# Gated delta rule in a hybrid backbone: z is projected with channels on partitions, its gate moves behind a transposition, and the products get a second kq buffer

## The chip, the cores and the metric

The kernel runs on one core of one Trainium2 chip. The metric is the device time of one execution in microseconds (us), as the median of several runs. The unchanged kernel took 2639.82 us (median of three runs, 2637.79 to 2641.33). The engines are called PE (matrix multiplication), PEld (its weight loads), DVE (vector), ACT (activation), POOL (GpSimd) and SP (which only issues DMAs here).

## The reference

Two layers over 2048 latent tokens and 256 context tokens of 1024 channels. The even layer has two branches behind one input projection: a bidirectional chunked gated delta rule (4 heads of 128 channels) and grouped attention. The change touches the delta rule's gate input z (columns 1536 to 2047 of the projection) and what multiplies it at the end:

```
pl = hl @ w_in
qkv_l, za_l, a_l, b_l, qb_l, kb_l, vb_l, zb_l = split_cols(pl, EVEN_SPLITS)
...
oa_l, _, _ = bidir_gdn(qa_l, ka_l, va_l, ga_l, ba_l, s_f, s_b, True)
...
def gdn_out(o, z, norm_g):
    bsz, nh, t, dv = o.shape
    o = rms_norm(o.transpose(0, 2, 1, 3), norm_g)
    y = o * jax.nn.silu(z.astype(F32).reshape(bsz, t, nh, dv))
    return y.reshape(bsz, t, nh * dv).astype(z.dtype)
```

## The kernel before

Every large product is split into a high and a low part and summed from three matmuls per 128 input channels (`mm3`, lines 133 to 138), so one output tile takes 24 of them.

The stages that matter follow each other in the program; a scheduler (the tile framework, with a timeline model of its own) then fixes one order of instructions per engine, and each engine works through its own list in that order. PE, for one, cannot pass over a matmul that waits.

**Projection "b"** (`b_item`, L517): tokens on partitions. 128 tokens are the stationary operand, 256 weight columns move. It is called for a/b/q, k, q and then for z: 2 column halves by 16 token tiles are 32 z items. A z item ends in Tanh on ACT (L554), a fused add and multiply on DVE (L555), the norm's gain `gg` on POOL (L557, tile zg) and a store to `d_zg` (L558).

**Projection "zb"** (`zb_item`, L604): the attention branch's gate, with channels on partitions. 128 weight columns are stationary, 512 tokens move; 4 heads by 4 token blocks are 16 items, each with Tanh (L612), DVE (L613) and a store.

**Products** (`gdn_products`, L785): for each of 18 chunks of 128 tokens (two of them context), what the recurrence needs and what does not depend on its state. For each direction d: two groups of four ACT scalings build gm from the high and the low part of the log decay (L796), two matmuls sum them into psg (L801, L802), four ACT exponentials give dm (L805), POOL masks it (L806). The matmuls of k with k and q (psk, L815) read tile kq, loaded from DRAM (L777), and DVE multiplies psk by dm into ntA and atA (L817, L819), which are stored. The ring of dm has two buffers, that of gm two, that of kq one. The products are emitted between the z items (`[prod] * 5` per item, L392).

**Substitution** (`gdn_subst`, L828): inverts 32 by 32 blocks of the chunks' triangular matrices, in 31 steps of one multiplication (sbT, L857) and one reduction on DVE (sbC, L858). Pass 0 runs on DVE; from pass 1 on, the steps after the twelfth multiply on POOL. Passes 0 and 1 are emitted beside z and zb, passes 2 to 4 (`late_subst`) beside attention. Pass 2 needs the last chunks' products.

**Mix** (`layer0_mix`, L619): attention, the recurrence (`gdn_chain`, L932, with `gdn_final`, L999) and the late substitution, merged. Attention starts with scores ps_s, which need khi (an ACT cast of the keys) and klo (DVE, L147). The keys' split lies in memory that the products release, and DVE casts three pieces of vhi ahead of klo. A final adds both directions' outputs (POOL, L1005), forms the norm, multiplies zg by it (POOL, L1015) and the output by that (POOL, L1016), transposes (PE, L1020), copies to yt (ACT, L1022) and stores. Tile yt shares a ring of three buffers ("ry") with r and y of the recurrence.

After that come the output projection, the second layer with its convolution, and its output; the change does not touch them.

Of the kernel before, what the change touches and what calls it, by code (L numbers as in the profile page):

```python
# [8 lines left out]
F32 = mybir.dt.float32  # L9
# [98 lines left out]
class Build:  # L108
# [44 lines left out]
    def setup(self, es):  # L153
# [29 lines left out]
        self.d_zg = d("d_zg", [NT, P, H * P])  # L183
# [103 lines left out]
    def layer0_in(self):  # L287
        tc, nc = self.tc, self.nc
        with ExitStack() as es:
# [67 lines left out]
            with tc.tile_pool(name="stB", bufs=2, reuse_waits="tile") as st:  # L357
                self.gq = st.tile([P, P], F32, name="gq", bufs=1)
                self.gk = st.tile([P, P], F32, name="gk", bufs=1)
                nc.sync.dma_start(self.gq, self.i["ev_q_norm_g"][0].partition_broadcast(P))  # L360
                nc.sync.dma_start(self.gk, self.i["ev_k_norm_g"][0].partition_broadcast(P))
                late = self.ada_late([(1, 4), (1, 5)], lambda: st.tile([P, 512], F32, tag="stage", name="ada_part2"))
                blks = [(2048, 272, "abq"), (2576, 256, "k"), (2320, 256, "q"), (1536, 256, "z")]
                items = []
                for (c0, n, kind), nxt in zip(blks, blks[1:]):
                    shared = {}
                    if kind == "q":
                        self.pipe(items)
                        items = []
                        e4.close()  # L370
                        self.es_mix = em = ExitStack()
                        cp = em.enter_context(tc.tile_pool(name="mixc", bufs=1, side="right", reuse_waits="tile"))
                        self.mix_consts(cp)
                        self.gg = cp.tile([P, P], F32, name="gg", bufs=1)
                        nc.sync.dma_start(self.gg, self.i["ev_gdn_norm_g"][0].partition_broadcast(P))
                        nc.vector.tensor_scalar(out=self.gg, in0=self.gg, scalar1=0.5, scalar2=None, op0=ALU.mult)
                        self.gates(cp)
                    for tt in range({"abq": NT + 1, "k": NTA}.get(kind, NT)):
                        items.append(self.b_item(c0, n, kind, tt, st, None, nxt[:2] if tt == 8 else None, shared))
                        if LATE_T(tt, kind):  # L380
                            items.append(late)
                self.pipe(items)
                self.pipe([late])
            with tc.tile_pool(name="stZ", bufs=2, reuse_waits="tile") as st:
                self.sub = em.enter_context(tc.tile_pool(name="subst", bufs=1, side="right", reuse_waits="tile"))
                with tc.tile_pool(name="prod", bufs=2, side="right", reuse_waits="tile") as gp:
                    prod = self.all_products(gp, self.tp)
                    subst = self.all_subst(range(2))
                    items = []
                    for c0, nxt in ((1536, (1792, 256)), (1792, (3088, P))):  # L390
                        for tt in range(NT):
                            items += [prod] * (0 if tt < Z_FREE and c0 == 1536 else 5) + [subst] * (SUB_Z if c0 > 1536 or tt >= 4 else 0)  # L392
# [124 lines left out]
    def b_item(self, c0, n, kind, tt, st, W=None, nxt=None, shared=None):  # L517
# [33 lines left out]
        if kind == "z":  # L551
            zs = st.tile([P, 2, P], F32, tag="wb", name="zs", bufs=4)
            z3 = body.rearrange("p (h c) -> p h c", h=2)
            nc.scalar.activation(zs, z3, AF.Tanh, scale=0.5)  # L554
            nc.vector.scalar_tensor_tensor(out=zs, in0=zs, scalar=1.0, in1=z3, op0=ALU.add, op1=ALU.mult)  # L555
            zg = st.tile([P, 2, P], F32, tag="wb", name="zg", bufs=4)
            nc.gpsimd.tensor_tensor(out=zg, in0=zs, in1=self.gg.unsqueeze(1).to_broadcast([P, 2, P]), op=ALU.mult)  # L557
            nc.sync.dma_start(self.d_zg[tt, :, c0 - 1536:c0 - 1536 + 256], zg)  # L558
            return
# [44 lines left out]
    def zb_item(self, hh, b, st, key, nxt):  # L604
# [9 lines left out]
        nc.sync.dma_start(self.d_szb[hh, :, b * 512:(b + 1) * 512], sz)  # L614
# [35 lines left out]
    def gates(self, cp):  # L650
# [134 lines left out]
    def gdn_products(self, c, gp, pp):  # L785
# [4 lines left out]
        for d in range(2):  # L790
# [7 lines left out]
            kq = kq or self.load_kq(c, gp, 1)  # L798
# [133 lines left out]
    def gdn_chain(self, d, c, n, W, done):  # L932
# [18 lines left out]
        else:  # L951
# [12 lines left out]
        nc.scalar.copy(y, py)  # L964
# [34 lines left out]
    def gdn_final(self, c, o):  # L999
# [4 lines left out]
        nc.sync.dma_start(zg, self.d_zg[c].rearrange("p (h c) -> p h c", h=H))  # L1004
# [10 lines left out]
        nc.gpsimd.tensor_tensor(out=zg, in0=zg, in1=rn.unsqueeze(2).to_broadcast([P, H, P]), op=ALU.mult)  # L1015
        nc.gpsimd.tensor_tensor(out=o, in0=o, in1=zg, op=ALU.mult)  # L1016
# [5 lines left out]
        nc.scalar.copy(yt, pt)  # L1022
# [517 lines left out]
```

## Time and profile before

| | us |
|---|---|
| median of three runs | 2639.82 |
| profiled execution, its own time | 2641.57 |
| its span | 2639.8 |
| first z Tanh (L554) starts | 637.2 |
| first zb weight load (L136, ps_zb) | 752.5 |
| first attention score (L136, ps_s) | 868.77 |
| last product of the recurrence's finals (L1016) starts | 1601.6 |
| last attention score starts | 1729.2 |

The profile page gives busy time, instructions and idle time by groups. A group's row reads: line, engine, operation, output<-inputs, shapes, count, then busy time and the mean duration of one in ns, then the engine's idle time just before these instructions and what ended most of it. Matmuls are pipelined: the duration of one reaches into the next one's, so two durations cannot be added; the distance from start to start can. A windows row gives for each engine the busy time and the count of instructions in a stretch, then the granted PE clock (1.00 is full speed), the DMA share and GB/s. A timeline row gives the start, the time from the first start to the last end of a run of equal instructions, the engine, the line, their count and in brackets the idle time before them.

### The profile page before, as it was taken

What the parts mean: (1) busy time and instruction counts of PE and PEld (TensorE: products, weight loads), DVE (VectorE), ACT (ScalarE), POOL (GpSimd) and SP (SyncE); (2) the same over time, 40 slices, a digit from 0 to 9 for tenths busy, and PEclk for the clock granted to TensorE, in tenths of its full rate; (3) what the DMA queues carried; (4) which work ended last, traced back from release to release, by engine and by line L of the source; (5) the groups of instructions that cost most, each with busy time, mean ns of one, the idle gap of its engine ahead of it and who ended that gap; (6) DMA issues with size and microseconds to landing.
All of it is one profiled execution on the core that took longest, in us unless ns stands there. A gap on an engine that the chain in (4) does not pass through costs nothing. (4 is left out here: it accounts for less than half of the span.)

```text
span 2639.8 us, 43225 instructions
## 1 busy us (share of the span) xinstructions
PE 2528.4 (96%) x15072; PEld 2206.1 (84%) x15072; DVE 2032.2 (77%) x4224; ACT 1457.2 (55%) x3033; POOL 1375.5 (52%) x1138
## 2 busy tenths in 40 slices
PE   7999999999999799999999999999999999999988
PEld 5888877998888688889989998887888888888767
DVE  8567667775855889897888777555489999997985
ACT  7444456224675665656566666444366667665332
POOL 3344433666445644361344324002179999897664
PEclk9999999999999899999999999999999999999989
DMA  8133334334566753545544434224311111116442
GB/s 313 49 122 101 109 112 130 107 102 152 164 195 203 202 122 109 147 116 139 158 116 129 125 96 132 63 81 142 136 49 56 56 60 61 56 64 213 151 158 100
DMA packets 372729, 323.21 MB, mean 122 GB/s; under 512 B 74784, under 2 KB 301600, under 8 KB 372512
## 3 DMA queue, kind: packets, MB, share of 16 engines
q1 hardware_dynamic: 372512, 320.46, 39.7%
q8 instruction: 119, 1.95, 0.3%
q14 instruction: 98, 0.80, 0.1%
HBM read 216.05 MB, written 104.33 MB: 121 GB/s over the span
## 5 line engine op out<-in xcount | busy, mean ns | idle before, releaser
L1410 DVE SCALAR_TENSOR_TENSOR pc<-u,hw,pc 128x1024 f32<-128x1024 f32 x320 | 389.7, 1280 | 5.1 <-ACT pc L1408 3.8
L1418 POOL TENSOR_TENSOR ac<-ac,pr 128x512 f32<-128x512 f32 x288 | 379.1, 1340 | 16.9 <-ACT ac L1414 6.2
L1121 ACT CAST phi<-pt 128x512 fp32r<-128x512 f32 x288 | 165.5, 585 | 157.1 <-PE pt L1117 145.3
L1417 ACT ACTIVATE pr<-u,hw 128x512 f32<-128x512 f32 x288 | 204.1, 721 | 84.8 <-POOL ac L1418 83.7
L1122 DVE TENSOR_TENSOR plo<-pt,phi 128x512 fp32r<-128x512 f32 x288 | 195.3, 685 | 60.0 <-ACT phi L1121 57.2
L136 PE MATMUL ps_b<-w_hi,hhi 128*128 128x256 f32 (+1 forms) x800 | 231.9, 292 | 9.6 <-DVE xn L571 6.1
L137 PE MATMUL ps_b<-w_lo,hhi 128*128 128x256 f32 (+1 forms) x800 | 228.0, 287 | 0.9 <-DVE w_lo L147 0.8
L138 PE MATMUL ps_b<-w_hi,hlo 128*128 128x256 f32 (+1 forms) x800 | 225.3, 287 | 0.6 <-POOL hlo L147 0.6
L1075 DVE TENSOR_SCALAR_CACHE_REDUCE S<-ps_s 128x512 f32<-128x512 f32 (+1 forms) x320 | 197.5, 630 | 23.3 <-PE ps_s L138 11.7
L1084 ACT ACTIVATE S<-S,m 128x1024 f32<-128x1024 f32 (+1 forms) x192 | 177.6, 928 | 61.3 <-DVE m L1081 60.8
L136 PE MATMUL ps_out<-wohi,yhi 128*128 128x512 f32 x512 | 204.2, 399 | 2.8 <-DVE x L1252 1.5
L138 PE MATMUL ps_out<-wohi,ylo 128*128 128x512 f32 x512 | 201.7, 395 | 0.7 <-DVE ylo L147 0.7
L137 PE MATMUL ps_out<-wolo,yhi 128*128 128x512 f32 x512 | 202.2, 395 | 0.0
L1145 PE MATMUL po<-phi,vhi 128*128 128x256 f32 x576 | 169.0, 315 | 12.4 <-ACT phi L1121 8.8
L1117 PE MATMUL pt<-ident,S 128*128 128x128 f32 x1152 | 174.1, 273 | 0.7 <-DVE plo L1122 0.5
L137 PE MATMUL ps_a<-hlo,w_hi 128*128 128x512 f32 (+1 forms) x448 | 170.7, 381 | 0.0
L136 PE MATMUL ps_a<-hhi,w_hi 128*128 128x512 f32 (+1 forms) x448 | 170.6, 381 | 0.0
L138 PE MATMUL ps_a<-hhi,w_lo 128*128 128x512 f32 (+1 forms) x448 | 170.1, 380 | 0.2 <-POOL w_lo L147 0.2
L477 DVE SCALAR_TENSOR_TENSOR acc<-ub,cols,acc 128x512 f32<-128x512 f32 (+1 forms) x168 | 136.5, 821 | 38.5 <-POOL acc L475 36.5
L136 PEld LDWEIGHTS ps_b<-w_hi,hhi 128*128 128x128 f32 x800 | 153.1, 192 | 13.1 <-issue 5.2
L857 POOL TENSOR_TENSOR sbT<-sbC 128x169 f32<-128x169 f32 (+18 forms) x76 | 120.2, 1582 | 77.9 <-DVE sbC L858 50.8
L137 PEld LDWEIGHTS ps_b<-w_lo,hhi 128*128 128x128 f32 x800 | 153.3, 192 | 2.4 <-DVE w_lo L147 1.8
(329 smaller groups left out, 7716.8 us busy)
## 6 DMA issues: line engine op xcount, KB each, us to landing
raw_ada<-in_ada_w_dram SPq DMA_DIRECT2D x48, 512.0 KB, 4.0
x<-in_x_dram SPq DMA_DIRECT2D x32, 512.0 KB, 7.7
kq<-d_kT SPq DMA_DIRECT2D x54, 256.0 KB, 3.4
raw_w<-in_ev_w_in_dram SPq DMA_DIRECT2D x26, 512.0 KB, 3.8
kq<-d_qT SPq DMA_DIRECT2D x48, 256.0 KB, 3.6
raw_w<-in_od_w_in_dram SPq DMA_DIRECT2D x24, 512.0 KB, 3.7
d_nt<-ntA SPq DMA_DIRECT2D x36, 256.0 KB, 3.3
nt<-d_nt SPq DMA_DIRECT2D x36, 256.0 KB, 4.4
```

Of the source, the lines that this page charges most:

```text
L136: self.nc.tensor.matmul(ps, lhsT=lh, rhs=rh, start=(a == 0), stop=False)
L137: self.nc.tensor.matmul(ps, lhsT=lh, rhs=rl, start=False, stop=False)
L138: self.nc.tensor.matmul(ps, lhsT=ll, rhs=rh, start=False, stop=(a == n - 1))
L1075: nc.vector.tensor_scalar(out=S[g][:, k0:k0 + w], in0=ps[:, :w], scalar1=1.0, scalar2=None, op0=ALU.mult, op1=ALU.max, accum_out=mx[:, b:b ...
L1084: nc.scalar.activation(S[g], S[g], AF.Exp, bias=m, scale=scale, accum_out=l[:, g:g + 1])
L1117: nc.tensor.transpose(pt[:, e, a * P:(a + 1) * P], S[a][k0 // 1024][:, k0 % 1024:k0 % 1024 + P], self.ident)
L1121: nc.scalar.copy(hi, pt)
L1122: nc.vector.tensor_tensor(out=lo, in0=pt, in1=hi.bitcast(F32), op=ALU.subtract)
L1145: nc.tensor.matmul(po, lhsT=vhi[:, ks], rhs=hi[:, e, :], start=(k == 0), stop=False)
L1410: nc.vector.scalar_tensor_tensor(out=pc, in0=s(j), scalar=w(j), in1=pc, op0=ALU.mult, op1=ALU.add)
L1417: nc.scalar.mul(pr, s(j), w(j))
L1418: nc.gpsimd.tensor_tensor(out=ac, in0=ac, in1=pr, op=ALU.add)
```

## The change

Four things are changed.

1. z is projected by `zb_item`, which takes its destination as an argument: 4 heads by 4 token blocks, 128 weight columns stationary and 512 tokens moving, 16 items in place of 32. `d_zg` holds channels by tokens. Between the items stand twice as many steps of the products and of the substitution. The norm's gain is no longer multiplied in here.
2. In `gdn_final` POOL multiplies o by the norm, PE transposes, ACT multiplies the transposed rows by the gain (now one value per partition) on its way out of PSUM, and POOL then multiplies yt by the gate.
3. kq has two buffers in the products.
4. Constants: the strict triangles are loaded apart and kept in one form, `negc` is gone (r takes the other sign, and y turns it back).

```diff
-        self.d_zg = d("d_zg", [NT, P, H * P])
+        self.d_zg = d("d_zg", [H, P, T])
...
-                    for c0, nxt in ((1536, (1792, 256)), (1792, (3088, P))):
-                        for tt in range(NT):
-                            items += [prod] * (0 if tt < Z_FREE and c0 == 1536 else 5) + [subst] * (SUB_Z if c0 > 1536 or tt >= 4 else 0)
-                            items.append(self.b_item(c0, 256, "z", tt, st, None, nxt if tt == 8 else None))
+                    zkey = [(1536 + hh * P, P) for hh in range(H)] + [(3088, P)]
+                    for n in range(4 * H):
+                        hh, b = n // 4, n % 4
+                        items += [prod] * (0 if n < 1 else 10) + [subst] * (2 * SUB_Z if n >= 2 else 0)
+                        items.append(self.zb_item(self.d_zg, hh, b, st, zkey[hh], zkey[hh + 1] if b == 2 else None))
...
-        if kind == "z":
-            zs = st.tile([P, 2, P], F32, tag="wb", name="zs", bufs=4)
-            z3 = body.rearrange("p (h c) -> p h c", h=2)
-            nc.scalar.activation(zs, z3, AF.Tanh, scale=0.5)
-            nc.vector.scalar_tensor_tensor(out=zs, in0=zs, scalar=1.0, in1=z3, op0=ALU.add, op1=ALU.mult)
-            zg = st.tile([P, 2, P], F32, tag="wb", name="zg", bufs=4)
-            nc.gpsimd.tensor_tensor(out=zg, in0=zs, in1=self.gg.unsqueeze(1).to_broadcast([P, 2, P]), op=ALU.mult)
-            nc.sync.dma_start(self.d_zg[tt, :, c0 - 1536:c0 - 1536 + 256], zg)
-            return
...
-            kq = kq or self.load_kq(c, gp, 1)
+            kq = kq or self.load_kq(c, gp, 2)
...
-                nc.vector.scalar_tensor_tensor(out=r[:, h, :], in0=pk[:, h, :], scalar=j(self.negc, h), in1=vt[:, h, :],
-                                               op0=ALU.mult, op1=ALU.add)
+                nc.vector.scalar_tensor_tensor(out=r[:, h, :], in0=pk[:, h, :], scalar=j(self.egc, h), in1=vt[:, h, :],
+                                               op0=ALU.mult, op1=ALU.subtract)
...
-        nc.scalar.copy(y, py)
+        nc.scalar.mul(y, py, 1.0 if S is None else -1.0)
...
-        nc.sync.dma_start(zg, self.d_zg[c].rearrange("p (h c) -> p h c", h=H))
+        nc.sync.dma_start(zg, self.d_zg[:, :, c * P:(c + 1) * P].rearrange("h p t -> p h t"))
...
-        nc.gpsimd.tensor_tensor(out=zg, in0=zg, in1=rn.unsqueeze(2).to_broadcast([P, H, P]), op=ALU.mult)
-        nc.gpsimd.tensor_tensor(out=o, in0=o, in1=zg, op=ALU.mult)
+        nc.gpsimd.tensor_tensor(out=o, in0=o, in1=rn.unsqueeze(2).to_broadcast([P, H, P]), op=ALU.mult)
...
-        nc.scalar.copy(yt, pt)
+        nc.scalar.mul(yt, pt, self.gg)
+        nc.gpsimd.tensor_tensor(out=yt, in0=yt, in1=zg, op=ALU.mult)
```

The edits move instructions on every engine's list. In the rows below a line number belongs to the version shown, and the numbers behind names tell buffers apart.

PE before, at the end of the stage: the last zb matmuls (ps_zb), then the last chunk's products (psg, psk) and attention's first scores (ps_s).

```order
L136 MATMUL ps_zb_10032<-hhi0_110,w_hi_9666 128x512
L802 MATMUL psg_9302<-gm_9257,strict_6329 128x512
L137 MATMUL ps_zb_10032<-hlo0_111,w_hi_9666 128x512
L138 MATMUL ps_zb_10032<-hhi0_110,w_lo_9667 128x512
L801 MATMUL psg_9321<-gm_9311,strict_6329 128x512
L815 MATMUL psk_9334<-kq_9262 128x256 x2
L815 MATMUL psk_9341<-kq_9262 128x256 x2
L802 MATMUL psg_9321<-gm_9316,strict_6329 128x512
L136 MATMUL ps_s_10127<-khi_9728,qhi_10121 128x512
```

PE now, from the last zb matmul on, down to the second of five chunks.

```order
L136 MATMUL ps_zb_9507<-hhi0_110,w_lo_9142 128x512
L793 MATMUL psg_8489<-gm_8481,strict_6329 128x512
L792 MATMUL psg_8508<-gm_8498,strict_6329 128x512
L806 MATMUL psk_8521<-kq_8486 128x256 x2
L806 MATMUL psk_8528<-kq_8486 128x256 x2
L793 MATMUL psg_8508<-gm_8503,strict_6329 128x512
L792 MATMUL psg_8552<-gm_8539,strict_6329 128x512
L793 MATMUL psg_8552<-gm_8544,strict_6329 128x512
L792 MATMUL psg_8618<-gm_8608,strict_6329 128x512
L806 MATMUL psk_8631<-kq_8549 128x256 x2
L806 MATMUL psk_8638<-kq_8549 128x256 x2
```

Before, two of the 72 psg matmuls and one of the 18 chunks' psk groups stood behind the last zb matmul. Now 19 psg matmuls and five psk groups stand there, and no projection lies between them. Ahead of that point, from the first psg on, each chunk's products have some 50 matmuls of 512 columns between them now; before, they had about 70 of 256 columns in z and 50 of 512 in zb.

ACT before, at the same place: the last two zb evacuations (szb), the last gm and dm groups, then the cast of the keys (khi).

```order
L612 ACTIVATE szb_10028<-ps_zb_10003 128x512
L796 ACTIVATE gm_9311<-cons_6327,ghi_6348 128x128 x4
L805 ACTIVATE dm_9305<-psg_9302,lnb_6343 128x128 x4
L796 ACTIVATE gm_9316<-cons_6327,glo_6349 128x128 x4
L612 ACTIVATE szb_10057<-ps_zb_10032 128x512
L805 ACTIVATE dm_9324<-psg_9321,lnb_6343 128x128 x4
L144 CAST khi_9728<-kraw_9730 128x1024
```

ACT now: the last szb and what follows it, and then the end of the same stretch.

```order
L602 ACTIVATE szb_9532<-ps_zb_9507 128x512
L796 ACTIVATE dm_8492<-psg_8489,lnb_6348 128x128 x4
L787 ACTIVATE gm_8503<-cons_6327,glo_6353 128x128 x4
L787 ACTIVATE gm_8539<-cons_6327,ghi_6352 128x128 x4
L796 ACTIVATE dm_8511<-psg_8508,lnb_6348 128x128 x4
L787 ACTIVATE gm_8544<-cons_6327,glo_6353 128x128 x4
```

```order
L851 COPY sbT_8164<-sbC_8163 128x1024
L796 ACTIVATE dm_8788<-psg_8785,lnb_6348 128x128 x4
L787 ACTIVATE gm_8821<-cons_6327,glo_6353 128x128 x4
L787 ACTIVATE gm_8879<-cons_6327,ghi_6352 128x128 x4
L796 ACTIVATE dm_8873<-psg_8870,lnb_6348 128x128 x4
L787 ACTIVATE gm_8884<-cons_6327,glo_6353 128x128 x4
L796 ACTIVATE dm_8892<-psg_8889,lnb_6348 128x128 x4
L840 ACTIVATE sbC_9621<-sbT_9622 64x1024
L142 CAST khi_9203<-kraw_9205 128x1024
```

Before, one dm group stood between the last szb and khi. Now ten dm groups, 17 gm groups, the copy at the end of substitution pass 1 (sbT<-sbC) and the first scaling of pass 2 (sbC<-sbT) stand there. POOL's list has, over the same stretch, dm and the last six multiplications of pass 1 (676 to 961 elements) in turn, then four dm.

POOL at a pair of finals, before: the norm (rno) and both multiplications, then the next W and the state's decay (S0, S1).

```order
L150 TENSOR_TENSOR rno_18780<-sso_18775,mhalf_64 128x4
L1015 TENSOR_TENSOR zgl_18771<-zgl_18771,rno_18780 128x512
L1016 TENSOR_TENSOR o_18472<-o_18472,zgl_18771 128x512
L150 TENSOR_TENSOR rno_18809<-sso_18804,mhalf_64 128x4
L881 TENSOR_TENSOR W_19321<-wc_19317,cons_6327 128x512
L1015 TENSOR_TENSOR zgl_18800<-zgl_18800,rno_18809 128x512
L1016 TENSOR_TENSOR o_18493<-o_18493,zgl_18800 128x512
L881 TENSOR_TENSOR W_19344<-wc_19340,cons_6327 128x512
L982 TENSOR_TENSOR S0_19804<-S0_19190,egt_6347 128x512
```

POOL now, at the same place.

```order
L148 TENSOR_TENSOR rno_18255<-sso_18250,mhalf_64 128x4
L1006 TENSOR_TENSOR o_17947<-o_17947,rno_18255 128x512
L148 TENSOR_TENSOR rno_18283<-sso_18278,mhalf_64 128x4
L872 TENSOR_TENSOR W_18796<-wc_18792,cons_6327 128x512
L1006 TENSOR_TENSOR o_17968<-o_17968,rno_18283 128x512
L872 TENSOR_TENSOR W_18819<-wc_18815,cons_6327 128x512
L1013 TENSOR_TENSOR yt_18465<-yt_18465,zgl_18246 128x512
L1013 TENSOR_TENSOR yt_18503<-yt_18503,zgl_18274 128x512
L973 TENSOR_TENSOR S0_19279<-S0_18665,egt_6351 128x512
```

The second multiplication of each final has moved behind the transposition and its copy, and stands right ahead of the state's decay.

More of the change, by code (lines that the diff above doesn't have):

```diff
@@ L49 @@
 for _name, _w in (
-    ("ident", 128), ("le", 128), ("gt", 128), ("ge", 128), ("lt", 128),
-    ("blk", 4),
+    ("ident", 128), ("le", 128), ("ge", 128), ("blk", 4), ("gt", 128), ("lt", 128),
 ):
@@ L373, in layer0_in @@
                         self.mix_consts(cp)
-                        self.gg = cp.tile([P, P], F32, name="gg", bufs=1)
-                        nc.sync.dma_start(self.gg, self.i["ev_gdn_norm_g"][0].partition_broadcast(P))
+                        self.gg = cp.tile([P, 1], F32, name="gg", bufs=1)
+                        nc.sync.dma_start(self.gg, self.i["ev_gdn_norm_g"][0].rearrange("(p o) -> p o", o=1))
                         nc.vector.tensor_scalar(out=self.gg, in0=self.gg, scalar1=0.5, scalar2=None, op0=ALU.mult)
@@ L405, in layer0_in @@
                     nxt = key[n] if 1 <= n < H else None
-                    items += [self.zb_item(hh, b, st, key[hh], nxt)] + [loadk] * (n >= 4)
+                    items += [self.zb_item(self.d_szb, hh, b, st, key[hh], nxt)] + [loadk] * (n >= 4)
                 self.pipe(items)
@@ L602, in b_item, with zb_item @@
             nc.sync.dma_start(dst[h0:h0 + 2, :, b * 512:b * 512 + w].rearrange("h p t -> p h t"), stage[:, :, :w])
-    def zb_item(self, hh, b, st, key, nxt):
+    def zb_item(self, dst, hh, b, st, key, nxt):
         nc = self.nc
@@ L613, in zb_item @@
         nc.vector.scalar_tensor_tensor(out=sz, in0=sz, scalar=1.0, in1=ps, op0=ALU.add, op1=ALU.mult)
-        nc.sync.dma_start(self.d_szb[hh, :, b * 512:(b + 1) * 512], sz)
+        nc.sync.dma_start(dst[hh, :, b * 512:(b + 1) * 512], sz)
         return
@@ L653, in gates @@
         g3 = lambda nm: cp.tile([P, NTA, 8], F32, name=nm)
-        self.g, self.lnb, self.egc, self.negc, self.kbs, self.egt = (
-            g3(nm) for nm in ("g", "lnb", "egc", "negc", "kbs", "egt"))
+        self.g, self.lnb, self.egc, self.kbs, self.egt = (g3(nm) for nm in ("g", "lnb", "egc", "kbs", "egt"))
         self.ghi, self.glo = (cp.tile([P, NTA, 8], F32R, name=nm) for nm in ("ghi", "glo"))
@@ L694, in gates @@
             ps = self.tp.tile([P, 3, NTA, 8], F32, tag="tp", name="ps_gate")
-            for d, (inc, rem) in enumerate((("le", "gt"), ("ge", "lt"))):
+            for d, inc in enumerate(("le", "ge")):
                 sl = slice(4 * d, 4 * d + 4)
                 nc.tensor.matmul(ps[:, 0, :, sl], lhsT=self.con(inc), rhs=self.g[:, :, sl], start=True, stop=True)
-                nc.tensor.matmul(ps[:, 1, :, sl], lhsT=self.con(rem), rhs=self.g[:, :, sl], start=True, stop=True)
+                nc.tensor.matmul(ps[:, 1, :, sl], lhsT=self.strict[:, d, :].bitcast(F32), rhs=self.g[:, :, sl], start=True, stop=True)
             nc.tensor.matmul(ps[:, 2, :, :], lhsT=self.ones, rhs=self.g, start=True, stop=True)
@@ L702, in gates @@
             nc.scalar.activation(self.egt, ps[:, 2, :, :], AF.Exp)
-            nc.vector.tensor_scalar(out=self.negc, in0=self.egc, scalar1=-1.0, scalar2=None, op0=ALU.mult)
             nc.vector.tensor_tensor(out=self.kbs, in0=self.kbs, in1=beta, op=ALU.mult)
@@ L707, in mix_consts @@
         nc = self.nc
-        self.cons = cp.tile([P, NCON - P], F32, name="cons")
-        nc.sync.dma_start(self.cons, self.i["cons"][:, P:])
+        n = NCON - 2 * P
+        self.cons = cp.tile([P, n - P], F32, name="cons")
+        nc.sync.dma_start(self.cons, self.i["cons"][:, P:n])
         self.strict = cp.tile([P, 2, P], F32R, name="strict")
-        for d, nm in enumerate(("gt", "lt")):
-            nc.scalar.copy(self.strict[:, d, :], self.con(nm))
+        with self.tc.tile_pool(name="mct", bufs=1, side="right", reuse_waits="tile") as tp:
+            raw = tp.tile([P, 2, P], F32, name="strict_raw")
+            nc.sync.dma_start(raw, self.i["cons"][:, n:].rearrange("p (a c) -> p a c", a=2))
+            nc.scalar.copy(self.strict, raw)
         dram = lambda nm, shape: self.dp.tile(shape, F32, name=nm)
```

5 lines of the change are left out of this document (2 added, 3 removed).

## The prediction

> **What bounds the kernel now.** I read the page's first part, then the windows around the stage that the change touches.
>
> ```profile
> PE 2528.4 (96%) x15072; PEld 2206.1 (84%) x15072; DVE 2032.2 (77%) x4224; ACT 1457.2 (55%) x3033; POOL 1375.5 (52%) x1138
> 633.00:752.00 119.00, 111.56 (x819) 105.84 (x818) 80.80 (x170) 86.35 (x278) 57.23 (x52) 0.99 0.54 160
> 752.00:861.00 109.00, 108.05 (x479) 89.16 (x479) 53.56 (x125) 69.83 (x206) 58.39 (x40) 1.00 0.70 202
> 861.00:868.00 7.00, 2.50 (x11) 1.58 (x9) 3.96 (x11) 3.92 (x14) 2.54 (x2) 0.96 0.67 228
> 868.00:881.00 13.00, 7.13 (x15) 4.17 (x15) 12.84 (x24) 4.67 (x6) 9.81 (x11) 0.50 0.64 152
> 900.00:1600.00 700.00, 675.01 (x5153) 633.74 (x5152) 592.83 (x1714) 432.34 (x1047) 288.86 (x251) 1.00 0.46 127
> ```
>
> PE bounds the kernel: it is busy for 96% of the span, for 111.56 of 119 us in the z stage, for 108.05 of 109 in zb and for 675 of 700 in attention. So an edit is worth what it takes from PE, less what it adds to PE's waits. PE waits most at the change from zb to attention (861 to 881), where the products must end before the keys are split.
>
> **PE's work in z.** Durations mislead here:
>
> ```profile
> L136 PE MATMUL ps_b<-w_hi,hhi 128*128 128x256 f32 x672 | 193.9, 291 | 8.7 <-DVE xn L571 5.3 <-DVE zs L555 1.7 <-ACT ada_part L1181 1.5
> L136 PE MATMUL ps_zb<-hhi,w_hi 128*128 128x512 f32 x128 | 51.2, 400 | 0.0
> 641.51 0.28 PE L136 MATMUL ps_b<-w_hi,hhi 128*128 128x256 f32 x1
> ...
> 644.75 0.28 PE L136 MATMUL ps_b<-w_hi,hhi 128*128 128x256 f32 x1
> ...
> 850.62 0.40 PE L136 MATMUL ps_zb<-hhi,w_hi 128*128 128x512 f32 x1
> ...
> 852.91 0.39 PE L137 MATMUL ps_zb<-hlo,w_hi 128*128 128x512 f32 x1
> ```
>
> A duration of 291 or 400 ns contains the part in which the next matmul already runs. From 641.51 to 644.75 lie 27 starts, so 256 columns cost 0.120 us; from 850.62 to 852.91 lie 10, so 512 columns cost 0.229 us. z is 32 x 24 = 768 matmuls at 0.120, 92.2 us; it becomes 16 x 24 = 384 at 0.229, 87.9 us. That is **4.3 us** less, not the 70 us that the durations promise (768 x 0.291 = 223 against 384 x 0.400 = 154).
>
> The Trainium skill ("TensorE: Matmul & The Clock Gate", Back-to-back issue gap) gives a sustained 131 ns for 512 columns and 81 ns for 128, far below 4 : 1. By it wide z would cost 50 us and the change would save some 25 us. The starts above, 0.229 against 0.120, do not bear that out.
>
> **Waits in z.** Of PE's 119 us there, 7.4 are idle, in zb 0.95 of 109. Most of them are psk waiting for DVE's atA, behind POOL's masks and its zg:
>
> ```profile
> POOL zg L557 <- DVE zs L555: 36.8, 18, 4.9
> DVE ntA L817 <- POOL dm L806: 23.4, 10, 4.7
> PE psk L815 <- DVE atA L819: 4.7, 4, 2.5
> ```
>
> The 32 zg on POOL go, and between two chunks' products now stand some 50 wide matmuls, as in zb. I let z run at zb's idle rate and take **6 us**; the bounds are 0 and 8.4, all the idle time of both windows. The second kq buffer helps the same waits and is in this figure. Tanh and the DVE step become half as many and less than twice as long, and four weight keys are split as before: all under a PE that is 99% busy.
>
> **What moves behind zb.** PE's list has 19 psg and five psk groups behind the last zb matmul, where 2 and one were. On PE a psk group is the eight starts from 848.21 to the next line's 849.75, 1.54 us:
>
> ```profile
> 848.21 1.89 PE L815 MATMUL psk<-kq 128*128 128x256 f32 x8
> 849.75 0.58 PE L136 MATMUL ps_zb<-hhi,w_hi 128*128 128x512 f32 x1
> ```
>
> So zb ends earlier by the 17 psg (17 x 0.229 = 3.9) and four psk groups (6.2) that left, and by the 4.3 and 6 above: **20.4 us**. This is no gain by itself, because attention waits for the products, and from there on they run without cover. Their price comes from ACT and POOL:
>
> ```profile
> 856.55 1.11 ACT L805 ACTIVATE dm<-psg,lnb 128x128 f32<-128x128 f32 x4
> 857.55 1.28 ACT L796 ACTIVATE gm<-cons,glo 128x128 fp32r<-128x128 f32 x4
> 858.73 0.59 ACT L612 ACTIVATE szb<-ps_zb 128x512 f32<-128x512 f32 x1
> L860 ACT COPY sbT<-sbC 128x1024 f32<-128x1024 f32 x1 | 2.1, 2133 | 1.7 <-DVE sbC L858 1.7
> 812.82 2.04 POOL L857 TENSOR_TENSOR sbT<-sbC 128x676 f32<-128x676 f32 x1 [0.95 <-DVE sbC L858]
> 814.81 1.30 POOL L806 TENSOR_TENSOR dm<-dm,cons 128x512 f32<-128x512 f32 x1
> ...
> 830.32 2.82 POOL L857 TENSOR_TENSOR sbT<-sbC 128x961 f32<-128x961 f32 x1
> L858 DVE TENSOR_REDUCE sbC<-sbT 128x31 f32<-128x961 f32 x1 | 1.1, 1142 | 0.0
> ```
>
> A gm group takes 1.18 us of ACT, a dm group 1.00. ACT alone needs 17 x 1.18 + 10 x 1.00 + 2.1 = 32.2 us. POOL is a little slower: six masks of 1.3 alternate with the last six multiplications of pass 1, which take 14.5 us (2.04 to 2.82; between 812.82 and 833.14 lie the six with three masks, 20.3 us). From the last zb matmul: psg 0.4, dm 1.0 and handing over 0.2 make 1.6; POOL's six pairs 22.3 make 23.9; the last reduction 1.1 and the copy 2.1 make 27.1; then ACT's dm, gm, gm, dm, gm, dm 5 x about 1.1 + 1.14 make 33.8; the mask 1.4 and DVE's four products 1.35 make **36.6 us**. One kq buffer would add a load to each chunk; two keep that off.
>
> Before, the same stretch and what follows it read:
>
> ```profile
> 861.11 1.89 PE L815 MATMUL psk<-kq 128*128 128x256 f32 x8
> 863.61 1.14 ACT L805 ACTIVATE dm<-psg,lnb 128x128 f32<-128x128 f32 x4 [0.15 <-issue]
> 867.18 0.41 DVE L819 TENSOR_TENSOR atA<-psk,dm 128x256 f32<-128x256 f32 x1
> 867.51 3.66 DVE L146 CAST vhi<-kvraw 128x1024 fp32r<-128x1024 f32 x3
> 867.68 1.99 ACT L144 CAST khi<-kraw 128x1024 fp32r<-128x1024 f32 x2 [2.93 <-issue]
> 868.77 1.22 PE L136 MATMUL ps_s<-khi,qhi 128*128 128x512 f32 x2 [5.26 <-ACT khi L144]
> 871.09 3.35 DVE L147 TENSOR_TENSOR klo<-kraw,khi 128x1024 fp32r<-128x1024 f32 x1
> ```
>
> zb ended at 861.1, the products at 867.6 and klo, which lets the scores run, began at 871.1, 10.0 us behind zb. Now the products end 36.6 behind it and vhi 40.3. On ACT the first scaling of pass 2 stands ahead of khi and waits for a load that SP issues behind the last chunk's stores: one direction before the end of the products (34), 2.3 us of issues, 3.5 us to landing, 1.06 us of scaling and 1.0 of khi give klo at about 42. **Sum:** attention starts 42 - 10.0 - 20.4 = 11.6 us later, and PE idles in that time.
>
> ```profile
> L849 ACT ACTIVATE sbC<-sbT 64x1024 f32<-64x1024 f32 x2 | 2.1, 1062 | 6.5 <-DMA sbT<-d_nt 3.8 <-DMA d_zg<-zg 2.7
> ```
>
> Bounds: the floor is ACT's 32.2 with 3.2 of start and drain and vhi, no wait of khi, and all 8.4 of idle regained: 39.1 - 10 - 22.8 = +6. The ceiling has nothing regained and a slow PE clock: in the window 868 to 881 it was 0.50 after the idle time, and psk groups at twice 1.54 would add some 3.5 us: 45.5 - 10 - 14.4 = +21. The Trainium skill (the same page, HAM oscillation) says that gaps of over about 3.4 us halve the clock; the 0.50 behind the 5.26 us gap agrees. It touches only that ceiling.
>
> **The finals.** POOL's 1.04 and 1.285 us stay, one on each side of the transposition:
>
> ```profile
> L1015 POOL TENSOR_TENSOR zgl<-zgl,rno x16: 1041/1042/1044, 1319.6 to 1600.5; 128x512 f32<-128x512 f32 x16
> L1016 POOL TENSOR_TENSOR o<-o,zgl x16: 1272/1285/1298, 1322.7 to 1601.6; 128x512 f32<-128x512 f32 x16
> POOL S L982 <- DVE S L984: 139.2, 11, 16.8
> ```
>
> I cost them at nothing: POOL is busy for 289 of 700 us there, waits for the state rather than the reverse (139.2 us in 11 waits), and the last final starts at 1601.6, with attention's scores running until 1729. The cover fails if yt's multiplication, which stands ahead of the state's decay on POOL, holds the recurrence up: at most 16 x 1.285 = 20.6 us; on the other side at most as much again could be regained of PE's 25 idle us there. ACT's scaling in place of the copy, the sign changes and the constants are one for one, and cost nothing.
>
> **The sum** is +11.6 us on the profiled execution (2641.57, of which 2639.8 are its span), 2653.2 there; on the median of 2639.82 it is **2651.4 us**. A measurement can tell about 0.2% of this kernel, 5.3 us, from no change.
>
> **Rivals.** (1) *Wide matmuls pay by duration.* Then z would shrink by up to 70 us, to about 2580. Starts of 0.229 and 0.120 us speak against it. Chance 0.03. (The Trainium skill's sustained spacing, above, is a milder form of this rival.) (2) *Faster:* the finals' transposition comes one POOL multiplication and one load earlier, and PE's list in attention waits less for the recurrence. The place is 900 to 1600, with 25.0 us of idle PE; from 11.6 + 5.3 = 17 us regained on, the kernel is faster, and all of it would give 2651.4 - 25 = 2626. For it: 16 x 1.285 us leave the chain ahead of the transposition. Against: the idle time is spread over many waits, and no long one names this tile. Chance 0.14. (3) *No difference:* the tail runs at its floor (+6) and some idle time goes: 2640 to 2645. Chance 0.18. (4) *Slower still:* the finals stall POOL ahead of the state's decay: up to 2651.4 + 20.6 = 2672. For it: POOL's list has yt right ahead of S0. Against: POOL's spare time. Chance 0.10. (5) *The second kq buffer changes nothing*, since PE sets the pace of the products; it is in the forecast.
>
> **How the numbers follow.** The forecast has 0.55, with its own range of +6 to +21, 2646 to 2661. Faster by over 0.2% is (1) and (2), 0.17; within it (3), 0.18; slower the forecast and (4), 0.65. The range of 2637 to 2664 leaves out (1), most of (2) and the upper part of (4), about 0.2.
>
> **What would show it.** z starts 0.229 us apart and PE without waits there; zb ending near 841 us; then a stretch of some 35 us in which PE is busy for a third and ACT and POOL nearly all the time; klo near 883; from there the same distance to the end. The forecast is wrong if the products keep up with zb on the chip, if the tail is far from 37 us, or if attention's idle time changes by over 10 us.

## The result

The changed kernel takes 2655.36 us (median of four runs, 2652.45 to 2656.05) against 2638.81 us of the kernel before beside it (2636.64 to 2641.33): ratio 1.0057, 95% interval 1.0042 to 1.0072, so 0.57% slower, some 15 us. The profiled execution has 2655.76 us and a span of 2654.0.

The page's first part, and windows by stage: z, zb, the tail (the products that stand behind the last zb matmul), the change to attention, attention.

```profile
PE 2540.3 (96%) x14688; PEld 2197.7 (83%) x14688; DVE 2023.7 (76%) x4205; ACT 1453.5 (55%) x3016; POOL 1353.2 (51%) x1108
625.00:734.00 109.00, 106.31 (x479) 87.39 (x478) 64.76 (x133) 61.43 (x177) 38.88 (x29) 1.00 0.50 148
734.00:843.00 109.00, 105.34 (x458) 86.77 (x457) 54.02 (x126) 64.79 (x198) 36.98 (x29) 0.98 0.62 183
843.00:884.00 41.00, 24.80 (x61) 16.55 (x59) 22.83 (x50) 32.85 (x110) 28.08 (x18) 0.68 0.73 205
884.00:891.00 7.00, 1.31 (x3) 0.59 (x3) 6.59 (x5) 2.98 (x4) 5.98 (x3) 0.50 0.50 115
900.00:1600.00 700.00, 675.38 (x5105) 632.24 (x5103) 587.46 (x1731) 433.26 (x1061) 295.63 (x259) 0.99 0.48 130
```

384 matmuls fewer, and PE is busy for 12 us more: in the stretch from 843 to 884 it works with a granted clock of 0.68, and ACT is the busy engine, for 32.85 of 41 us. Attention is as before (675 of 700).

PE's timeline at zb's end, in the tail and at the start of attention:

```profile
840.67 0.39 PE L135 MATMUL ps_zb<-hlo,w_hi 128*128 128x512 f32 x1
...
842.94 0.40 PE L136 MATMUL ps_zb<-hhi,w_lo 128*128 128x512 f32 x1
...
843.63 1.89 PE L806 MATMUL psk<-kq 128*128 128x256 f32 x8
...
858.45 0.80 PE L792 MATMUL psg<-gm,strict 128*128 128x512 f32 x1 [0.63 <-ACT gm L787]
859.04 3.62 PE L806 MATMUL psk<-kq 128*128 128x256 f32 x8
862.09 0.99 PE L793 MATMUL psg<-gm,strict 128*128 128x512 f32 x1
...
874.12 0.50 PE L793 MATMUL psg<-gm,strict 128*128 128x512 f32 x1 [2.53 <-ACT gm L787]
...
878.93 0.99 PE L793 MATMUL psg<-gm,strict 128*128 128x512 f32 x1
887.98 1.22 PE L134 MATMUL ps_s<-khi,qhi 128*128 128x512 f32 x2 [8.06 <-ACT khi L142]
890.91 0.79 PE L135 MATMUL ps_s<-klo,qhi 128*128 128x512 f32 x1 [1.71 <-DVE klo L145]
```

Between 840.67 and 842.94 lie ten starts, 0.227 us each. The last zb matmul starts at 842.94; the first score that needs klo starts 48.0 us later, where it was 13.9 (860.6 to 874.5).

ACT's timeline in the same stretch, then DVE's:

```profile
843.87 1.14 ACT L796 ACTIVATE dm<-psg,lnb 128x128 f32<-128x128 f32 x4
...
854.93 1.14 ACT L796 ACTIVATE dm<-psg,lnb 128x128 f32<-128x128 f32 x4 [0.92 <-issue]
...
860.46 1.29 ACT L787 ACTIVATE gm<-cons,ghi 128x128 fp32r<-128x128 f32 x4
863.17 1.14 ACT L796 ACTIVATE dm<-psg,lnb 128x128 f32<-128x128 f32 x4 [1.42 <-issue]
...
876.09 1.33 ACT L787 ACTIVATE gm<-cons,glo 128x128 fp32r<-128x128 f32 x4
880.01 1.14 ACT L796 ACTIVATE dm<-psg,lnb 128x128 f32<-128x128 f32 x4 [2.59 <-issue]
885.93 1.06 ACT L840 ACTIVATE sbC<-sbT 64x1024 f32<-64x1024 f32 x1 [4.78 <-DMA sbT<-d_nt]
886.90 1.98 ACT L142 CAST khi<-kraw 128x1024 fp32r<-128x1024 f32 x2
```

```profile
883.91 3.64 DVE L144 CAST vhi<-kvraw 128x1024 fp32r<-128x1024 f32 x3
887.96 4.57 DVE L145 TENSOR_TENSOR klo<-kraw,khi 128x1024 fp32r<-128x1024 f32 x2 [0.41 <-ACT khi L142]
```

dm at 863.17 needs the psg matmul of 862.09, which stands behind psk of 859.04 in PE's list. So the rows put the pauses called "issue" behind psk: 3.05 us from psk's start to the next line's, where 1.54 had been counted. As an estimate, with 1.54 us and 0.4 for the psg behind it, the three psg would have ended at about 853.2, 861.0 and 877.8, and ACT was done with its gm at 854.0, 861.8 and 877.4: nearly all of the pauses would be gone.

### The profile page after: what moved, and what is told of

It is laid out like the page before. It is cut to its first block, busy times and chain, and to the rows that moved or that the text cites. A ratio compares the mean times of both kernels' runs of the same rounds, so it can differ in the third digit from the quotient of the medians.

```text
span 2654.0 us, 42356 instructions
## 1 busy us (share of the span) xinstructions
PE 2540.3 (96%) x14688; PEld 2197.7 (83%) x14688; DVE 2023.7 (76%) x4205; ACT 1453.5 (55%) x3016; POOL 1353.2 (51%) x1108
## 5 line engine op out<-in xcount | busy, mean ns | idle before, releaser
L1066 DVE TENSOR_SCALAR_CACHE_REDUCE S<-ps_s 128x512 f32<-128x512 f32 (+1 forms) x320 | 197.7, 630 | 32.3 <-PE ps_s L136 15.9
L134 PE MATMUL ps_out<-wohi,yhi 128*128 128x512 f32 x512 | 204.0, 398 | 2.4 <-DVE yhi L144 1.3
L136 PE MATMUL ps_out<-wohi,ylo 128*128 128x512 f32 x512 | 201.3, 394 | 0.6 <-DVE ylo L145 0.5
L1136 PE MATMUL po<-phi,vhi 128*128 128x256 f32 x576 | 170.8, 318 | 11.1 <-ACT phi L1112 7.3
L136 PE MATMUL ps_a<-hhi,w_lo 128*128 128x512 f32 (+1 forms) x448 | 171.3, 382 | 0.7 <-POOL w_lo L145 0.7
L134 PE MATMUL ps_a<-hhi,w_hi 128*128 128x512 f32 (+1 forms) x448 | 171.6, 383 | 0.0
L134 PE MATMUL ps_b<-w_hi,hhi 128*128 128x256 f32 (+1 forms) x544 | 157.6, 293 | 6.6 <-DVE xn L561 6.5
L135 PE MATMUL ps_b<-w_lo,hhi 128*128 128x256 f32 (+1 forms) x544 | 154.1, 286 | 0.0
L136 PE MATMUL ps_b<-w_hi,hlo 128*128 128x256 f32 (+1 forms) x544 | 152.7, 288 | 0.6 <-POOL hlo L145 0.6
L1137 PE MATMUL po<-phi,vlo 128*128 128x256 f32 x576 | 151.4, 284 | 0.0
L134 PE MATMUL ps_s<-khi,qhi 128*128 128x512 f32 (+1 forms) x320 | 135.4, 424 | 11.7 <-ACT khi L142 8.1
```

The lines of the kernel that those rows point to most:

```text
L134: self.nc.tensor.matmul(ps, lhsT=lh, rhs=rh, start=(a == 0), stop=False)
L135: self.nc.tensor.matmul(ps, lhsT=lh, rhs=rl, start=False, stop=False)
L136: self.nc.tensor.matmul(ps, lhsT=ll, rhs=rh, start=False, stop=(a == n - 1))
L1066: nc.vector.tensor_scalar(out=S[g][:, k0:k0 + w], in0=ps[:, :w], scalar1=1.0, scalar2=None, op0=ALU.mult, op1=ALU.max, accum_out=mx[:, b:b ...
L1136: nc.tensor.matmul(po, lhsT=vhi[:, ks], rhs=hi[:, e, :], start=(k == 0), stop=False)
```

## The experiments

All numbers of the table are from the profiled executions. A: start of projection "a"'s last matmul of both high parts (the row of ps_a at L134 or L136; "a" stands ahead of all that the edits touch) to that of the last zb matmul, for before 860.6 - 444.3. B: from there to the first score with klo. C: from there to the start of the last output matmul. Last, the ratio to the kernel before, timed beside it, with its 95% interval. The starts are given to a tenth, so a difference can be 0.1 off.

| kernel | A | B | C | ratio |
|---|---|---|---|---|
| before | 416.3 | 13.9 | 1756.6 | 1 |
| changed | 395.5 | 48.0 | 1754.4 | 1.0057 (1.0042 to 1.0072) |
| kq1 | 395.6 | 49.2 | 1756.3 | 1.0046 (1.0030 to 1.0061) |
| old_finals | 396.2 | 47.8 | 1759.7 | 1.0055 (1.0042 to 1.0069) |
| new_finals | 415.4 | 13.8 | 1756.5 | 0.9986 (0.9977 to 0.9994) |
| gm3 | 415.6 | 0.4 | 1762.8 | 0.9971 (0.9962 to 0.9981) |
| b_gm3 | 418.1 | 0.5 | 1761.6 | 0.9982 (0.9973 to 0.9991) |
| p0 | 387.2 | 47.7 | 1753.3 | 1.0016 (1.0007 to 1.0025) |
| b_p0 | 405.9 | 18.2 | 1764.1 | 1.0009 (1.0000 to 1.0018) |
| gm3_p0 | 405.0 | 0.4 | 1758.6 | 0.9915 (0.9902 to 0.9928) |
| gm3_dm3_p0 | 409.5 | 0.5 | 1758.1 | 0.9916 (0.9903 to 0.9929) |
| b_gm3_p0 | 405.7 | 0.5 | 1752.9 | 0.9899 (0.9883 to 0.9915) |
| half_psk | 385.4 | 48.4 | 1755.3 | 1.0001 (0.9992 to 1.0010) |

Each row is one execution. A and B repeat well: the changed kernel and kq1, whose lists differ in loads alone, are 0.1 and 1.2 us apart. But 27 executions of the kernel before took 2634.19 to 2646.11 us, so a difference of less than some 5 us in C says nothing by itself.

**kq1: one kq buffer again.**

```diff
-            kq = kq or self.load_kq(c, gp, 2)
+            kq = kq or self.load_kq(c, gp, 1)
```

> The changed kernel with one kq buffer in the products again; PE, ACT, DVE and POOL keep their lists, only loads move on SP's. The theory of the tail (the loss comes from the 19 psg and five psk groups behind the last zb matmul): they are still there, so 2655 us, within 5 us; the loads are hidden by some 8 us of ACT work per chunk. The rival that the second kq buffer does harm (loads on SP's queue ahead of stores): back towards 2639, and the stretch from zb's end to klo falls from 44.9 to under 38 us.

2654.98 us; A, B and C as in the changed kernel. The second kq buffer neither helps nor harms here.

**gm3: the tail taken away.** The scheduler's list depends on gm's ring: with three buffers, PE's has no product behind zb.

```diff
-                t = gp.tile([P, H, P], F32R, tag="gm", name="gm", bufs=2)
+                t = gp.tile([P, H, P], F32R, tag="gm", name="gm", bufs=3)
...
-            kq = kq or self.load_kq(c, gp, 2)
+            kq = kq or self.load_kq(c, gp, 1)
```

> The changed kernel with three gm buffers (and one kq buffer, so that they fit). In PE's list no psg and no psk stands behind the last zb matmul any more, the products end some 140 matmuls ahead of it. Theory of the tail: zb ends about 12 us later (19 x 0.229 + 5 x 1.54) than 843, at about 855, the scores follow within 1 us in place of 44.9, so attention starts 30 to 35 us earlier: 2618 to 2628 us, under both kernels. The rival of the finals (they cost the time): 2650 to 2656, nothing changes. The rival that ACT and POOL cannot keep the products up with PE: waits of psg and psk of 10 to 25 us in the z stage, 2630 to 2645.

2634.8 us: faster than the kernel before, and 0.75% faster than kq1, from which it differs in gm's ring alone. B fell from 48.0 to 0.4 as expected. The time missed the expectation by 7 us, since zb ended 20 us later, not 12 (the products that came back take 15 us by their starts, and PE idles 3 us more), and C is 8 us longer. It lies in the range of the rival in which the products cannot keep up with PE, and psk does wait for 9.1 us in z and zb, a little under that rival's 10 to 25. So the tail is the loss, and a smaller one lies in the z stage. Windows of gm3:

```profile
640.00:840.00 200.00, 190.77 (x824) 155.92 (x823) 128.36 (x271) 153.41 (x473) 90.02 (x61) 0.97 0.69 200
700.00:720.00 20.00, 16.90 (x71) 13.58 (x70) 19.79 (x33) 13.37 (x44) 6.62 (x5) 0.94 0.57 169
720.00:740.00 20.00, 19.00 (x82) 15.37 (x80) 19.79 (x26) 11.34 (x39) 5.17 (x3) 0.98 0.59 173
```

PE idles 9.2 us; from 700 to 740 DVE, not ACT or POOL, is the full engine, busy for 39.6 of 40 us, and POOL for 11.8. DVE multiplies pass 0 of the substitution there.

**b_gm3: the same on the kernel before** (`bufs=3` in gm's line above, nothing else).

> The kernel before with three gm buffers and nothing else; no product stands behind the last zb matmul there either. Theory of the tail: the 13.4 us between zb's end (861.1) and the scores that need klo (874.5) shrink to 1, and two psg and one psk group (2 us) move ahead of zb's end: about 10 us less, 2628 us. The distance from this to the changed kernel with three gm buffers is then what the wide z is worth by itself, 4 to 10 us. Rival (a third buffer buys nothing where two had no tail): 2636 to 2640.

2637.14 us. B fell from 13.9 to 0.5 and A rose by 1.8, both as expected, but C is 5 us longer, and the 10 us shrank to 5 against the kernel before beside it (2642.0). The time lies in the rival's range, though the interval leaves a gain of 0.09% to 0.27%. The point for the main question: with no tail in either, the wide z (0.9971) is no slower than the narrow one (0.9982), so the loss of the changed kernel needs the tail.

**old_finals: the changed kernel without the finals' part.**

```diff
-        nc.gpsimd.tensor_tensor(out=o, in0=o, in1=rn.unsqueeze(2).to_broadcast([P, H, P]), op=ALU.mult)
+        nc.gpsimd.tensor_tensor(out=zg, in0=zg, in1=rn.unsqueeze(2).to_broadcast([P, H, P]), op=ALU.mult)
+        nc.gpsimd.tensor_tensor(out=o, in0=o, in1=zg, op=ALU.mult)
...
-        nc.scalar.mul(yt, pt, self.gg)
-        nc.gpsimd.tensor_tensor(out=yt, in0=yt, in1=zg, op=ALU.mult)
+        nc.scalar.copy(yt, pt)
```

> The changed kernel with the finals in their old order (POOL multiplies the gate by the norm, then o by that; PE transposes; ACT copies); the gate is read in its new layout and the gain is left out, so the values are others, and the work of the old finals is done. PE's list around zb is the changed kernel's, tail included. Theory of the tail: 2655 us, within 5. The rival that the new finals stall POOL and the recurrence: 2639 to 2648, and less PE idle time between 900 and 1600. If the new finals gain something: up to 2665.

2657.48 us: the loss stays when the new finals go.

**new_finals: the kernel before with the finals' part alone** (the reverse edit, with `self.gg[:, 0:1]`).

> The kernel before with only the finals in their new order (POOL multiplies o by the norm, PE transposes, ACT scales by one value per partition, POOL multiplies by the gate as z stored it); the gate is read in its old layout, so the values are others, and the work is that of the new finals. PE's list around zb is that of before. Theory of the tail: 2639 us, within 4. If the finals carry the loss: 2646 to 2656. If they carry a hidden gain (the changed kernel with the old finals was 2.5 us slower than with the new): 2635 to 2638.

2639.89 us beside 2643.88 of before: the finals cost nothing, and by the interval (0.06% to 0.23% faster) they may gain a little.

**p0: pass 0's late multiplications on POOL, in the changed kernel.**

```diff
-SUB_POOL = (1, 2, 3, 4)
+SUB_POOL = (0, 1, 2, 3, 4)
```

> The changed kernel with pass 0's late multiplications on POOL and nothing else: two gm buffers, so 19 psg and five psk groups still stand behind the last zb matmul. Theory of the tail: the tail stays at 40 to 42 us and the scores that need klo come 47 to 50 us behind the last zb matmul's start; only PE's idle time in z (7 us between 640 and 840) can go: 2647 to 2655 us. Rival (pass 0 on POOL is what made the version with three gm buffers fast, not the tail's removal): 2625 to 2640.

2643.74 us, 3 us under the expected range, while the tail stayed as expected. The windows of p0, z and zb, then its tail:

```profile
622.00:831.00 209.00, 209.00 (x933) 172.94 (x932) 94.29 (x239) 126.87 (x374) 101.31 (x76) 1.00 0.59 172
840.00:880.00 40.00, 21.45 (x49) 13.98 (x49) 24.29 (x42) 28.54 (x86) 27.46 (x18) 0.67 0.68 184
```

PE is busy for the whole of z and zb, zb ends 8.3 us earlier than in the changed kernel, and the tail (B 47.7, clock 0.67) stays. So the tail and DVE's multiplications are two separate losses.

**b_p0: the same on the kernel before.**

> The kernel before with pass 0's late multiplications on POOL and nothing else; three psg and one psk group stand behind the last zb matmul. It lost 7.4 us of PE time in z, mostly in psk's waits for DVE. If these were DVE's multiplications of pass 0: 5 to 7 us less, 2633 to 2637, and the 13.4 us from zb's end to klo's scores stay. Rival (both edits are needed): within 2 us of 2640.

2642.74 us, not the 2633 to 2637 expected, and 3 us from the rival's 2640: A fell by 10.4 us, but B rose by 4.3 and C by 7.5. The waits in z were DVE's, and the gain was lost behind them.

**gm3_p0 and gm3_dm3_p0: both edits in the changed kernel,** then three dm buffers as well (`bufs=3` in dm's line).

> The changed kernel with three gm buffers, one kq buffer, and the late multiplications of substitution pass 0 on POOL as in the other passes (DVE keeps the reductions). With three gm buffers PE idled 9.2 us between 640 and 840, in waits of psk for DVE, which at 700 to 740 was 99% busy with pass 0's multiplications while POOL had 12 of 40 us. If DVE's list is the cause: idle time in that stretch under 4 us, and 2628 to 2631 us. Rival (POOL's longer multiplications hold up the masks as they did in the tail): idle time of 8 us or more, 2633 to 2640.

> As the kernel before this one, with three dm buffers as well, so that ACT's exponentials do not wait for DVE to release dm (2.5 to 5.6 us each between 700 and 740 with two). If that wait reaches PE, the idle time between 640 and 840 falls by 1 to 3 us against it and the time is 2626 to 2630; if only DVE's pace counts, the two agree within 2 us.

2621.03 and 2620.72 us: 0.85% under the kernel before. gm3_p0 is 7 us under its expected range; the two agree within 2 us, as expected if DVE's pace alone counts. In gm3_p0 PE's idle time from 640 to 840 fell from 9.2 to 3.8 us, as expected if DVE's list is the cause. The third dm buffer adds nothing to the time. In its profiled execution, the slowest of six, PE idles 6.1 us there, and most of it is one wait for a load of kq, of which these versions have one buffer:

```profile
PE psk L806 <- DMA kq<-d_qT: 4.4, 1, 4.4
```

**b_gm3_p0: both edits on the kernel before.**

> The kernel before with three gm buffers and pass 0's late multiplications on POOL. Its z has POOL's zg as well, so POOL is the fuller engine here. With three gm buffers alone it took 2637.1 us. If DVE's list held its products too: 2632 to 2636; if POOL now does: 2637 to 2642. Its distance to the changed kernel with the same two edits is what the wide z and the finals are worth where no tail is left; by matmul starts 4.3 us.

2616.4 us, the fastest of all, and far from the expected 2632 to 2642, which had counted z's waits and the tail but not that C, 1752.9, comes back to its old length when both are gone. Windows of gm3_p0, then of b_gm3_p0:

```profile
640.00:840.00 200.00, 196.17 (x872) 162.08 (x871) 107.24 (x257) 157.41 (x476) 116.90 (x79) 1.00 0.71 206
```

```profile
640.00:840.00 200.00, 199.40 (x1200) 179.60 (x1200) 111.05 (x275) 151.80 (x476) 138.55 (x109) 1.00 0.71 206
```

In these windows the narrow z leaves PE 0.6 us of idle time and the wide z 3.8. But the narrow z starts at 620.4 and idles for 2.5 us ahead of 640; from z's first matmul to zb's last PE idles 3.1 us with the narrow z and 3.8 with the wide. From start to next start, without idle time, the wide z takes 5.6 us less than the narrow. The matmuls of zb, psk and psg take 3.0 us more beside it, and PE idles 1.8 us more over the whole of A, so that only 0.7 stay in A (405.7 against 405.0). In C the wide version is 5.7 us longer, little more than C's scatter. The two intervals overlap: a gain of the wide z without a tail is neither shown nor excluded.

**half_psk: psk's half left out, in the changed kernel.**

```diff
-        m = 2 if lat else 1
+        m = 1
...
-                    nc.vector.tensor_tensor(out=ats[d][:, e:e + 2, :], in0=psk[:, :, 1, :], in1=dms[d][:, e:e + 2, :],
+                    nc.vector.tensor_tensor(out=ats[d][:, e:e + 2, :], in0=psk[:, :, 0, :], in1=dms[d][:, e:e + 2, :],
```

> The changed kernel with psk halved: the product of k and q is left out and atA is formed from the product of k and k, so psk is 128 columns in place of 256 and PE has half of it to do; ACT, POOL and DVE do what they did. 21 psg and five psk groups stand behind the last zb matmul, one direction more than before the edit. In the tail of the changed kernel ACT paused for 0.92, 1.42 and 2.59 us, each time behind a psk group that took 3.05 us at a halved PE clock in place of 1.54. If these pauses are psk's: they sum to under 1.5 us now, psk groups take about 1.5 us at the halved clock, and the tail (from the last zb matmul to the last atA) is 36.6 + 3.4 (the direction more) = 40 us at most. Rival (the pauses are waits for POOL's masks or for gm's ring): they stay at 4 to 6 us and the tail is 44 us. Time: 2640 to 2650, since 18 psk groups are 0.77 us shorter in z and zb.

2641.35 us. PE in the tail of half_psk, then ACT there:

```profile
836.64 2.07 PE L806 MATMUL psk<-kq 128*128 128x128 f32 x8 [2.77 <-DVE atA L810]
...
850.02 1.91 PE L806 MATMUL psk<-kq 128*128 128x128 f32 x8
851.61 0.80 PE L793 MATMUL psg<-gm,strict 128*128 128x512 f32 x1
```

```profile
839.22 1.14 ACT L796 ACTIVATE dm<-psg,lnb 128x128 f32<-128x128 f32 x4 [2.86 <-PE psg L793]
...
865.94 1.14 ACT L796 ACTIVATE dm<-psg,lnb 128x128 f32<-128x128 f32 x4 [0.98 <-POOL sbT L848]
866.96 1.97 ACT L851 COPY sbT<-sbC 128x1024 f32<-128x1024 f32 x1
```

psk takes 1.59 us at the halved clock, and between 839.22 and 865.94 ACT no longer pauses behind it. But psk itself waited 2.77 us for atA at the tail's start, which stopped ACT for 2.86, and the pauses still sum to 3.8 us. So the expectation held for the pauses behind psk's own work and not in its sum: the tail is 41.5 us to the end of the last atA, not 40. That psk at the halved clock made the changed kernel's pauses is supported; that these 4.9 us would be won without it isn't shown.

## Why the prediction was right, and where it was off

**What z costs on PE: right in kind, too small in size.** Wide matmuls start 0.227 us apart, not 0.400; they pay by starts. But the 0.120 us came from 27 starts without a break. Over the whole stage, from start to next start without idle time, z's 768 narrow matmuls took 95.9 us (0.125 each) and its 384 wide ones 89.4 (0.233 each): 6.5 us less, not 4.3. The sustained 131 ns that the Trainium skill gives ("TensorE: Matmul & The Clock Gate", Back-to-back issue gap) does not show here either.

**The waits in z: wrong in what removes them.** The step was that z between the products, now with some 50 wide matmuls, would idle like zb, 6 us less. From z's first matmul to zb's last PE idled 9.6 us before and idles 6.4 now, 3.3 less. In the changed kernel psk still waits for atA, as PE's waits from 625 to 842 show, with the longest of them; beside them the DVE and POOL rows ahead of it:

```profile
PE psk L806 <- DVE atA L810: 6.4, 3, 3.7
745.51 3.40 PE L806 MATMUL psk<-kq 128*128 128x256 f32 x8 [3.66 <-DVE atA L810]
```

```profile
732.09 3.97 DVE L848 TENSOR_TENSOR sbT<-sbC 64x841 f32<-64x841 f32 x1
...
738.36 1.84 DVE L848 TENSOR_TENSOR sbT<-sbC 64x900 f32<-64x900 f32 x1
```

```profile
732.05 2.41 POOL L145 TENSOR_TENSOR w_lo<-raw_w,w_hi 128x1024 fp32r<-128x1024 f32 x1 [4.11 <-ACT w_hi L142]
```

The prediction blamed POOL's masks and zg. Taking zg away left these waits; taking pass 0's multiplications from DVE (p0) ended them. Yet zb's end came 20.8 us earlier against 20.4 forecast. That is luck, for two terms missed in opposite directions: the matmuls that moved behind zb took 9.8 us with them (10.1 forecast), z itself became 6.5 shorter (4.3 forecast), and PE's idle time fell by 4.4 over the whole of A (6 forecast), 1.1 of it ahead of z.

**The tail: right in kind, 4.5 us short.** Its length by ACT and POOL was counted as 36.6 us; from the start of the last zb matmul to the end of the last atA it is 41.1. The term that failed is psk, taken at 1.54 us and beside ACT's work. At the halved clock it takes 3.05 and delays the next psg, on which ACT waits: 0.92 + 1.42 + 2.59 us of pauses. From 843.87 to the last dm's end at 881.15 ACT has 32.3 us of work, as counted (32.2), and these pauses, and nothing else. So ACT, not POOL's pairs, set the length. The slow clock stood in the ceiling only. That the tail itself is the loss is shown by gm3 against kq1 (ratio 0.9971 against 1.0046) and by gm3 against b_gm3.

**klo at 42 behind zb's end: about 45** (887.96 - 842.94). The 4.5 us of the tail are in it. The wait of khi for pass 2's load is there (4.78 us), but DVE, casting vhi until 887.55, would have started klo only 0.41 us earlier without it; the wait was foreseen rightly, but what sets klo's start is the products' end and vhi. The 10.0 us of before were counted from zb's end, the 42 from its last matmul's start; from the same point, before has 10.4.

**The finals at nothing: held,** from both sides (old_finals, new_finals). ACT's scaling isn't one for one with the copy, though; the rows of the changed kernel and of the kernel before:

```profile
L1012 ACT ACTIVATE yt<-pt,gg x16: 682/688/704, 1325.6 to 1608.7; 128x512 f32<-128x512 f32 x16
```

```profile
L1022 ACT COPY yt<-pt x16: 562/586/609, 1325.7 to 1606.6; 128x512 f32<-128x512 f32 x16
```

That is 0.10 us more, 16 times, under cover. Rival 5 (the second kq buffer changes nothing) held as well (kq1).

**The sum.** +11.6 us was forecast, 2651.4 us with a range of 2646 to 2661, and 2655.36 was measured. In the profiles A gives -20.8, B +34.1 and C -2.2, +11.1 together; the span grew by 14.2, because this execution was 3.1 us late already at the last matmul of "a" (447.4 against 444.3; kq1 445.1, p0 444.2 with the same work ahead). By the ratio it is 11 to 19 us. That +11.1 comes so near to +11.6 is partly luck too: klo comes 45 us behind zb's last matmul, not 42, and C, which the forecast left unchanged, is 2.2 us shorter, within its scatter. The direction and the path (zb earlier, the products uncovered on ACT and POOL, attention later) are no luck.

**Open.** C differs by up to 11 us between versions (1752.9 to 1764.1) that change little in attention's work but the lists of the engines. For gm3, b_gm3 and b_p0 it is more than scatter: by their medians, against the kernel before beside them, they end 7 to 8 us later than A and B alone would give. In gm3 and b_gm3 PE idles for 54 us of C, against 49 in the kernel before and 45 in the changed one; in b_p0 PE is not idle for longer but busy for longer, 1714 us against 1708. What in the lists makes that so is not known.

## What to carry to other kernels

Making the bounding engine's stage shorter gains nothing where other work was hidden under it: ask what still has to finish before the next stage, on which engine, and where the scheduler will put it. Here one more buffer in the ring of gm brought 19 psg matmuls and five psk groups back under cover and turned a loss of 0.46% (kq1) into a gain of 0.29% (gm3); with DVE's multiplications moved to POOL, which had time to spare, the gain was 0.85%, and without the wide z no less (1.01%). A wait's releaser in the profile (here DVE's atA) is only the last step: read what stood ahead of it in its engine's list.

## What the hardware showed that was not expected

The clock was granted at 0.68 in a tail whose idle gaps on PE, up to 879, were at most 2.53 us. It first fell between 851 and 855, when no gap had been longer than 1.69 us:

```profile
849.55 0.50 PE L793 MATMUL psg<-gm,strict 128*128 128x512 f32 x1 [1.69 <-ACT gm L787]
846.00:851.00 5.00, 1.78 (x4) 0.84 (x5) 3.70 (x9) 5.00 (x19) 5.00 (x4) 0.98 0.74 229
851.00:855.00 4.00, 4.00 (x11) 2.97 (x10) 2.51 (x6) 3.08 (x12) 4.00 (x3) 0.60 0.42 133
```

The prediction used the rule of gaps over 3.4 us; such gaps were not needed here. The same page of the Trainium skill ("TensorE: Matmul & The Clock Gate", A second HAM failure mode: psum-queue depth-cycling) tells of frequent short idle times between groups of matmuls that make the clock swing, and the tail agrees with that.

DVE's multiplication of 64x841 at 732.09 took 3.97 us, beside 1.84 for the larger 64x900 six microseconds later; POOL's w_lo ran from 732.05 for 2.41 us at the same time. The Trainium skill ("SBUF — State Buffer", SBUF: two separate sides) says that a DVE operation with two inputs in that memory and a POOL operation that reads it exclude each other for a whole instruction. The traces agree. Below is the same multiplication in the kernel before, with no POOL operation beside it, and in gm3, where POOL's mask starts with it:

```profile
723.98 1.75 DVE L857 TENSOR_TENSOR sbT<-sbC 64x841 f32<-64x841 f32 x1
```

```profile
732.18 2.91 DVE L848 TENSOR_TENSOR sbT<-sbC 64x841 f32<-64x841 f32 x1
732.18 1.29 POOL L797 TENSOR_TENSOR dm<-dm,cons 128x512 f32<-128x512 f32 x1 [2.55 <-DVE sbC L849]
```

Less POOL's 2.41 and 1.29 us, the slow ones have 1.56 and 1.62 us left, near the 1.75 without company. It goes the other way as well: in the changed kernel POOL's mask at 734.82, begun while DVE still multiplied, took 2.42 us, and the one at 748.45 took 1.29. No experiment changed this alone.
